# A row gradient on one core: six rows per partition over three tiles, and slots at multiples of 256 bytes

## The chip, the core and the metric

The kernel runs on one core of a Trainium2 chip. The metric is the device time of one execution in microseconds (us). Before the change the median of three runs was 1247.84 us, from 1247.62 to 1248.39.

## What is computed

The input is an 8192 x 8192 array of 32-bit floats. Each row is differentiated by itself:

```python
"x": np.random.randn(8192, 8192).astype(np.float32)

def reference(x):
    return np.gradient(x, axis=1)
```

Inside a row, the result at column j is half of x[j+1] - x[j-1]. At the two ends of a row it is the plain difference of the two outermost elements. 268.4 MB go in and 268.4 MB come out, and each element is used only within its own row.

## The kernel before

Memory on the core (SBUF) has 128 partitions. The 8192 rows are cut into 32 sets of 256 consecutive rows; each partition holds two consecutive rows of a set, 64 KiB that are contiguous in memory (HBM). The views of lines 36 and 37 do this cut: partition p of set s has rows 256 s + 2 p and 256 s + 2 p + 1. So the 128 pieces of one transfer lie end to end, and a transfer covers 8 MiB.

There are three slots in SBUF (line 40), each with 64 + 16,384 elements per partition. A set is loaded at element 64 of its slot (line 60). VectorE then writes half the difference of the neighbours to the same slot, 64 elements further down (line 76), so that it overwrites only what it has read. It runs over both rows as one stretch and leaves four wrong elements, at the ends of the two rows. GpSimd has put the right ones aside before (line 70, tile `ends`), and a small copy on VectorE or GpSimd sets them in place (line 87). The result is stored from element 0 of the slot (line 89).

All 64 transfers are issued by SyncE, in program order. Three loads come first. After each third set, the loads of the next three sets are issued (lines 91 to 93); each waits for the store that frees its slot (line 61). The order of SyncE is therefore: three stores, three loads, three stores, and so on; ten groups of three sets and a last one of two. The order of all engines is the one written out, and `chain` (line 45) names, for each instruction, the steps that it needs; other waits inside a slot are dropped as implied.

In the built program the first slot starts at byte 16,512 of each partition, which is 64 x 256 + 128; a slot is 65,792 bytes, 257 x 256, so the other two start 128 bytes past a multiple of 256 too.

Of the kernel before, what the change touches and what calls it, by code (L numbers as in the profile page):

```python
# [1 line left out]

# [4 lines left out]


@with_exitstack
def kernel(  # L10
    ctx: ExitStack,
    tc: tile.TileContext,
    x: bass.AP,
    out: bass.AP,
):

    nc = tc.nc
    P = nc.NUM_PARTITIONS
    n, m = x.shape
    R = 2
    NB = 3  # L30
    SH = 64
    W = R * m
    nsets = n // (P * R)
    f32 = x.dtype

    x_sets = x.rearrange("(s p t) m -> s p (t m)", p=P, t=R)
    out_sets = out.rearrange("(s p t) m -> s p (t m)", p=P, t=R)

    pool = ctx.enter_context(tc.tile_pool(name="pool", bufs=1))
    slots = [pool.tile([P, SH + W], f32, name=f"slot{k}", tag=f"slot{k}") for k in range(NB)]  # L40
    ends = pool.tile([P, nsets, R, 2], f32, name="ends", tag="ends")
    loads, stores = [], [None] * nsets
    in_front = {}

    def chain(i, ins, *needed):

        group, engine = f"slot{i % NB}", ins.ins.engine
        keep = [o.ins for o in needed]  # L50
        if in_front.get(engine, (None,))[0] == group:
            keep.append(in_front[engine][1])
        tc.declare_no_dep(ins.ins, group=group, keep=keep, reason="implied by the needed step")
        tc.add_to_no_dep_group(group, ins.ins)
        in_front[engine] = group, ins.ins
        return ins

    def load(i):
        b = slots[i % NB]
        ins = nc.sync.dma_start(out=b[:, SH : SH + W], in_=x_sets[i])  # L60
        loads.append(chain(i, ins, *([stores[i - NB]] if i >= NB else [])))

    with tc.manual_schedule():
        for i in range(NB):
            load(i)
        for i in range(nsets):
            b = slots[i % NB]
            xin = b[:, SH : SH + W].rearrange("p (t m) -> p t m", m=m)

            ins = nc.gpsimd.tensor_sub(  # L70
                out=ends[:, i, :, :],
                in0=xin[:, :, 1 : m : m - 2],
                in1=xin[:, :, 0 : m - 1 : m - 2],
            )
            at = [chain(i, ins, loads[i])]
            ins = nc.vector._custom_dve(  # L76
                dve_ops.TENSOR_TENSOR_REDUCE_SUB_MAX,
                out=b[:, 1 : W - 1],
                in0=b[:, SH + 2 : SH + W],
                in1=b[:, SH : SH + W - 2],  # L80
                s0=0.0,
                s1=0.5,
            )
            halved = chain(i, ins, *at)
            res = b[:, 0:W].rearrange("p (t m) -> p t m", m=m)
            placer = nc.gpsimd if i % 5 in (1, 3) and i < nsets - 2 else nc.vector
            ins = placer.tensor_copy(out=res[:, :, 0 : m : m - 1], in_=ends[:, i, :, :])  # L87
            placed = chain(i, ins, halved)
            ins = nc.sync.dma_start(out=out_sets[i], in_=b[:, 0:W])
            stores[i] = chain(i, ins, placed)  # L90
            if i % NB == NB - 1:
                for k in range(i + 1, min(i + 1 + NB, nsets)):
                    load(k)


# [1 line left out]
_INS = ['x']  # L97
_OUTS = [((8192, 8192), 'float32')]


# [23 lines left out]
```

## Time and profile before

| | us |
|---|---|
| median of three runs | 1247.84 |
| span of the profiled execution | 1245.7 |
| VectorE busy | 554.6 (45%) |
| GpSimd busy | 8.8 (1%) |
| one long VectorE operation (line 76) | 17.224 |
| one subtraction on GpSimd (line 70) | 0.198 |
| one copy of line 87 on VectorE, on GpSimd | 0.172, 0.190 |
| a load from issue to landing, median | 58.0 |
| a store from issue to landing, median | 40.4 |

The span runs from the first to the last instruction of the profiled execution, and the median of the runs is 2.1 us longer. The profile names engines as DVE (VectorE), POOL (GpSimd) and SP (SyncE); SPq is SyncE's queue of transfers. The time from issue to landing holds the wait behind the transfers that were issued earlier, since all share the same 16 DMA engines.

### The profile page before, as it was taken

The numbers are of one execution on the slowest core, as the hardware profiler recorded it, in microseconds if no ns is written. First come the engines' busy times: TensorE is split into PE (matmuls) and PEld (weight loads), VectorE is DVE, ScalarE is ACT, GpSimd is POOL, SyncE is SP. The second block draws the span as 40 slices with busy tenths as digits, with TensorE's granted clock in tenths as the row PEclk, the third lists the DMA queues.
The fourth block names the chain that finished last, engine by engine and source line by source line (L and its number), as shares of the span: only waits on it lengthen the run. The fifth ranks groups of instructions, "written<-read, shape, count | busy, mean of one in ns | idle before, by whom it ended". The sixth has DMA issues, their size and how long they took to land.

```text
span 1245.7 us, 237 instructions
## 1 busy us (share of the span) xinstructions
DVE 554.6 (45%) x52; POOL 8.8 (1%) x48
## 2 busy tenths in 40 slices
DVE  2850583069009702850582079009603840591083
POOL 0000000000000000000000000000000000000000
DMA  9999999999999999999999999999999999999999
GB/s 404 438 436 423 427 431 438 438 438 436 436 427 431 425 438 436 425 434 436 429 434 436 434 436 434 436 434 438 419 436 436 434 438 438 431 434 429 429 410 404
DMA packets 9217, 536.88 MB, mean 431 GB/s; under 512 B 1024, under 2 KB 1024, under 8 KB 1024
## 3 DMA queue, kind: packets, MB, share of 16 engines
q1 hardware_dynamic: 9216, 536.88, 99.8%
q14 instruction: 1, 0.01, 0.0%
HBM read 268.44 MB, written 268.44 MB: 431 GB/s over the span
## 4 chain that ended last, share of the span: by engine, by line
another core or an unknown queue 74%; DVE 18%; DMA 3%; issue 2%; POOL 1%; SPq 0%; POOLq 0%
DVE slot L76 18%; DMA slot<-in_x_dram 3%; POOL ends L70 0%; POOL slot L87 0%; SPq L60 0%; POOLq L119 0%; DVE slot L87 0%
## 5 line engine op out<-in xcount | busy, mean ns | idle before, releaser
L76 DVE CUSTOM_DVE_ANT_0 slot<-slot 128x16382 f32<-128x16382 f32 x32 | 551.2, 17224 | 668.7 <-POOL ends L70 668.7
L70 POOL TENSOR_TENSOR ends<-slot 128x4 f32<-128x4 f32 x32 | 6.3, 198 | 989.6 <-DMA slot<-in_x_dram 989.6
L87 POOL COPY slot<-ends 128x4 f32<-128x4 f32 x12 | 2.3, 190 | 207.9 <-DVE slot L76 207.9
L87 DVE COPY slot<-ends 128x4 f32<-128x4 f32 x20 | 3.4, 172 | 0.7
L108 POOL MEMSET const-bfloat16-1.0<- 128x1 bf16 x1 | 0.1, 101 | 0.0
L108 POOL MEMSET const-uint8-127<- 128x1 uint8 x1 | 0.1, 101 | 0.0
L108 POOL MEMSET const-float32-0.0<- 128x1 f32 x1 | 0.1, 98 | 0.2 <-issue 0.2
L108 POOL MEMSET const-float32-1.0<- 128x1 f32 x1 | 0.1, 98 | 0.0
## 6 DMA issues: line engine op xcount, KB each, us to landing
slot<-in_x_dram SPq DMA_DIRECT2D x32, 58.0
out_dram<-slot SPq DMA_DIRECT2D x32, 40.4
```

What stands on the lines that cost most here:

```text
L70: ins = nc.gpsimd.tensor_sub(out=ends[:, i, :, :], in0=xin[:, :, 1 : m : m - 2], in1=xin[:, :, 0 : m - 1 : m - 2],)
L76: ins = nc.vector._custom_dve(dve_ops.TENSOR_TENSOR_REDUCE_SUB_MAX, out=b[:, 1 : W - 1], in0=b[:, SH + 2 : SH + W], in1=b[:, SH : SH + W - 2],
L87: ins = placer.tensor_copy(out=res[:, :, 0 : m : m - 1], in_=ends[:, i, :, :])
L108: nc = _bacc.Bacc("TRN2", target_bir_lowering=False, num_devices=1)
```

## The change

The views of lines 36 and 37 are replaced by a function that cuts the rows in groups of three sets. A group is 768 consecutive rows, and each partition has six consecutive ones, 192 KiB. The first set of the group takes the first two rows of each partition, the second the next two, the third the last two. A transfer still moves 64 KiB for each of 128 partitions; its pieces now stand 192 KiB apart. The last group has two sets, with four rows per partition and a pitch of 128 KiB. The same cut is used for input and output.

A tile of 32 elements (128 bytes) per partition is placed ahead of the slots. Nothing reads or writes it. The first slot then starts at byte 16,640, 65 x 256, and the other two at multiples of 256 as well.

```diff
-    x_sets = x.rearrange("(s p t) m -> s p (t m)", p=P, t=R)
-    out_sets = out.rearrange("(s p t) m -> s p (t m)", p=P, t=R)
+    def sets(a):
+        found = []
+        for first in range(0, nsets, NB):
+            q = min(NB, nsets - first)
+            rows = a[first * P * R : (first + q) * P * R, :].rearrange("(p q) m -> p (q m)", p=P)
+            found += [rows[:, k * W : (k + 1) * W] for k in range(q)]
+        return found
+
+    x_sets, out_sets = sets(x), sets(out)
 
     pool = ctx.enter_context(tc.tile_pool(name="pool", bufs=1))
+    pad = pool.tile([P, 32], f32, name="pad", tag="pad")
     slots = [pool.tile([P, SH + W], f32, name=f"slot{k}", tag=f"slot{k}") for k in range(NB)]
```

## The prediction

> **What bounds the kernel now.** I read the page first, then SyncE's waits, then the timeline.
>
> ```profile
> DVE 554.6 (45%) x52; POOL 8.8 (1%) x48
> ...
> GB/s 404 438 436 423 427 431 438 438 438 436 436 427 431 425 438 436 425 434 436 429 434 436 434 436 434 436 434 438 419 436 436 434 438 438 431 434 429 429 410 404
> DMA packets 9217, 536.88 MB, mean 431 GB/s; under 512 B 1024, under 2 KB 1024, under 8 KB 1024
> ...
> q1 hardware_dynamic: 9216, 536.88, 99.8%
> ...
> another core or an unknown queue 74%; DVE 18%; DMA 3%; issue 2%; POOL 1%; SPq 0%; POOLq 0%
> ```
>
> The 16 DMA engines are occupied for 99.8% of the span, VectorE for 45%. The 74% that the chain of waits puts on an unknown queue is waiting for transfers. 9216 less 1024 small packets are 8192 of 64 KiB: 64 transfers x 128 partitions, one packet per partition and transfer.
>
> The timeline follows (start, time, engine, line, operation, idle time before it). The GpSimd subtraction of line 70 waits for a load, so its start marks a landing.
>
> ```profile
> 22.71 0.20 POOL L70 TENSOR_TENSOR ends<-slot 128x4 f32<-128x4 f32 x1 [22.27 <-DMA slot<-in_x_dram]
> ...
> 42.04 0.20 POOL L70 TENSOR_TENSOR ends<-slot 128x4 f32<-128x4 f32 x1 [19.13 <-DMA slot<-in_x_dram]
> ...
> 62.44 0.20 POOL L70 TENSOR_TENSOR ends<-slot 128x4 f32<-128x4 f32 x1 [2.69 <-DMA slot<-in_x_dram]
> ...
> 411.86 0.20 POOL L70 TENSOR_TENSOR ends<-slot 128x4 f32<-128x4 f32 x1 [19.85 <-DMA slot<-in_x_dram]
> ...
> 489.13 0.20 POOL L70 TENSOR_TENSOR ends<-slot 128x4 f32<-128x4 f32 x1 [59.56 <-DMA slot<-in_x_dram]
> ...
> 974.22 0.20 POOL L70 TENSOR_TENSOR ends<-slot 128x4 f32<-128x4 f32 x1 [19.15 <-DMA slot<-in_x_dram]
> 974.45 17.22 DVE L76 CUSTOM_DVE_ANT_0 slot<-slot 128x16382 f32<-128x16382 f32 x1 [1.92 <-POOL ends L70]
> 991.71 0.17 DVE L87 COPY slot<-ends 128x4 f32<-128x4 f32 x1
> 993.55 0.20 POOL L70 TENSOR_TENSOR ends<-slot 128x4 f32<-128x4 f32 x1 [19.13 <-DMA slot<-in_x_dram]
> ...
> 1206.28 0.20 POOL L70 TENSOR_TENSOR ends<-slot 128x4 f32<-128x4 f32 x1 [19.14 <-DMA slot<-in_x_dram]
> ```
>
> Two loads in a row land 993.55 - 974.22 = 19.33 us apart. Between 411.86 and 489.13 three stores and a load pass: 77.27 / 4 = 19.32 each. So loads and stores have one rate: 8.389 MB / 19.32 us = 434 GB/s. The compute of a set (0.20 + 17.22 + 0.17 us) fits beside one transfer, with the 1.92 us that VectorE idles to spare.
>
> This splits the profiled execution. 64 x 19.32 = 1236.5 us is pure transfer. Of the 1245.7 us span 9.2 are left: the first landing is 22.71 - 19.32 = 3.39 late (start); from there to the last landing 61 transfers should take 1178.5 us and take 1206.28 - 22.71 = 1183.57, 5.05 more; the two stores behind it should take 38.64 and take 1245.7 - 1206.28 = 39.42, 0.78 more. Most of the 5.05 sits in one place, the third load of each group, after which the queue turns from reading to writing: 62.44 - 42.04 = 20.40 us is 1.08 over 19.32. Over the ten full groups these excesses are 1.08, 0.13, 0.19, 0.73, 0.53, 0.47, 0.13, 0.52, 0.01 and 0.04, in all 3.8 us; the stretches of three stores and a load exceed 77.28 by about 1.0 in all, the second loads 19.32 by 0.25. Around the span lie 1247.84 - 1245.7 = 2.1 us that I carry over to the median.
>
> **What the change does, part by part.** The instructions stay: 32 loads, 32 stores, 32 subtractions, 32 long VectorE operations, 32 copies; the pad is written by none. The 64 issues by SyncE stay too, in their order.
>
> ```profile
> SPq L89 <- DVE slot L87: 525.6, 20, 55.9
> SPq L60 <- DMA out_dram<-slot: 373.1, 29, 19.3
> ```
>
> SyncE spends its time waiting for results and landed stores (us, times, longest), while a transfer or two still lie in the queue; an issue (0.34 us) is hidden behind them and would cost 64 x 0.34 = 22 us with that cover gone. Bytes per packet and packets per transfer stay as well. Two things move.
>
> First, **slot alignment**. A slot is 65,792 bytes, 257 x 256; the first starts at byte 16,512 of its partition, 128 past a multiple of 256. So now the SBUF side of every load and store is shifted by half of 256 bytes, and the pad (32 x 4 bytes) takes that away. The trace has no unshifted transfer, so bounds: if the shift costs nothing, 0. If it makes each packet pay for 128 bytes more, 128 / 65,536 of 1236.5 us, 2.4 us. That loads and stores both take 19.32 fits either end, since both touch the shifted side. A reason for a loss I don't see: a packet on a boundary has no piece more. I take the middle, -1.2.
>
> The Trainium skill ("DMA: Bandwidth & Descriptors", How a descriptor splits into AXI transactions) says that a read not starting on a multiple of 256 bytes begins at the boundary below and pays for the unused bytes. Its rule charges the read side, so stores alone, and by it the estimate would be half of the upper bound, 1.2 us. Equal rows for loads and stores speak against a charge on one side alone.
>
> Second, **row pitch**. A transfer's 128 pieces of 64 KiB lay end to end in HBM; now they stand 192 KiB apart and three transfers fill the gaps (the last group has two, pitch 128 KiB). A transfer's addresses then span 24 MiB, not 8. In the middle of a stretch of one direction nothing shows HBM as the limit: 19.32 us comes back for loads and stores, at the start and the end of the run. So I cost the steady stretches at 0. Where reads meet writes (the third load, the 3.8 us) the place in HBM can matter: now the last load of a group and the first store lie two sets, 16 MiB, apart in their tensors, then 128 KiB. Bounds: all 3.8 gone, or the stumble of the first group, 1.08, at all ten: 10.8 - 3.8 = +7.0. The present stumbles run from 0.01 to 1.08 at one pitch, so most of it has to do with how the engines happen to stand to one another, not with the addresses; the typical row (0.13 to 0.5) is nearer to none than to 1.08. I take -1.0, about a quarter of 3.8.
>
> Sum: 1245.7 - 1.2 - 1.0 = 1243.5 us of span, + 2.1 = **1245.6 us**.
>
> A gain at the third loads isn't eaten later: the queue has work until the last group, so a shorter third load lets every later landing move up. What is late next is the store of set 30, issued when its load has landed and 17.6 us of compute are done; both move up with it.
>
> **The rivals.**
>
> (a) The turnarounds go smooth: nearly all of the 3.8 vanishes, with 1.2 from alignment: 1247.84 - 5.0 = 1242.8 us. For it: reads and writes then differ in low address bits. Against: four groups already have under 0.15 without it.
>
> (b) Nothing that decides is touched: the 19.32 is the engines' own rate and the stumbles are chance: 1247.8 us. For it: the one rate in both directions. Against: only that two things do change on the path that sets the time.
>
> (c) Slower: the wider pitch puts the 16 streams in each other's way in HBM. Its place is the turn from loads to stores; priced as the first group's, 1.08 at each of ten, it gives 1247.84 + 7.0 = 1254.8 us. It decides, beyond 0.2%, from (3.8 + 2.5) / 10 = 0.63 us each, or in the steady stretch from 19.32 to 19.36 us per transfer (2.5 / 64 = 0.04). For it: stumbles of 1.08, 0.73 and 0.53 show that engines can hold each other up. Against: no steady stretch shows it.
>
> The Trainium skill ("DMA: Bandwidth & Descriptors", Latency and other measured facts, HBM row pitch) reports copies at a 512 KiB pitch at 207 GB/s per direction, 164 at 2 MiB, 103 at 4 MiB, against 214 at full rate. Were 192 KiB to cost what 512 KiB does there, the estimate would be 1236.5 x 7 / 207 = 42 us more; the present 64 KiB pitch runs without loss here, and no run shows a wider one.
>
> (d) Also slower: the row ranges of three stores now interleave, and if the program takes them as overlapping, each waits for the one before. The shortest store took 20.9 us from issue to landing, so 20.9 - 19.32 = 1.6 us of empty queue at two stores of each of ten groups and one of the last: 21 x 1.6 = 34 us, 1281 us. Against: the kernel names its waits, and only input, compute and slot are among them.
>
> **How the numbers follow.** My forecast 42%, (a) 23%, (b) 16%, (c) 15%, (d) 4%. A measurement of this kernel can tell about 0.2%, 2.5 us, from no change: faster is below 1245.3, slower above 1250.3. The forecast's own range, 1244.0 to 1247.5, lies on both sides: 18% of its 42 faster, 24 same. Faster 18 + 23 = 41%, same 24 + 16 = 40%, slower 19%. The range goes from 1241.5 ((a) with the upper bound of alignment, 1247.84 - 3.8 - 2.4 = 1241.6) to 1250.5, which leaves out most of (c), all of (d).
>
> **What would show it.** Landings of two loads in a row: 19.33 now; 19.29 if alignment is worth its full 2.4 us (2.4 / 64 = 0.04), 19.32 if nothing, over 19.36 if the pitch hurts. Third loads: the sum of their excess, 3.8 now, 2.8 by the forecast, near 0 by (a), 10 by (c). SyncE's waits of line 89 on a landed store would show (d). I am wrong in kind if the steady 19.32 moves by more than 0.04, and wrong in size if the third loads carry more than the 3.8 they have.

## The result: 1.9 us less, and the profile after

The changed kernel takes 1246.27 us (median of 21 runs, 1245.23 to 1247.13); the kernel before took 1248.16 us in the 21 runs beside them. The ratio is 0.9985, with a 95% interval from 0.9979 to 0.9991: a small gain, about 1.9 us. It is inside the 0.2% that the prediction counted as no change, but the interval does not reach 1, so the gain is real. The profiled execution has a span of 1244.3 us, 1.4 less than the one before.

The page of the changed kernel, with the lines that answer to those of before:

```profile
DVE 554.6 (45%) x52; POOL 8.9 (1%) x48
...
GB/s 404 438 436 423 421 438 438 438 438 436 434 423 430 434 438 438 430 436 432 428 434 436 432 436 434 438 436 430 432 428 438 436 434 438 434 434 430 430 409 404
DMA packets 9217, 536.88 MB, mean 431 GB/s; under 512 B 1024, under 2 KB 1024, under 8 KB 1024
...
q1 hardware_dynamic: 9216, 536.88, 99.8%
...
another core or an unknown queue 74%; DVE 18%; DMA 3%; issue 2%; POOL 1%; SPq 0%; POOLq 0%
```

Nothing has changed in kind: the same packets, the same work on the engines, the DMA engines occupied for 99.8%. The gain is too small for this page, so the landings have to be read one by one. The timeline of the changed kernel (start, time, engine, line, operation, idle time before it); what was line 70 is line 65 now:

```profile
22.77 0.20 POOL L65 TENSOR_TENSOR ends<-slot 128x4 f32<-128x4 f32 x1 [22.32 <-DMA slot<-in_x_dram]
...
42.03 0.20 POOL L65 TENSOR_TENSOR ends<-slot 128x4 f32<-128x4 f32 x1 [19.07 <-DMA slot<-in_x_dram]
...
62.34 0.20 POOL L65 TENSOR_TENSOR ends<-slot 128x4 f32<-128x4 f32 x1 [2.60 <-DMA slot<-in_x_dram]
...
410.87 0.20 POOL L65 TENSOR_TENSOR ends<-slot 128x4 f32<-128x4 f32 x1 [19.41 <-DMA slot<-in_x_dram]
...
488.16 0.20 POOL L65 TENSOR_TENSOR ends<-slot 128x4 f32<-128x4 f32 x1 [59.58 <-DMA slot<-in_x_dram]
...
972.75 0.20 POOL L65 TENSOR_TENSOR ends<-slot 128x4 f32<-128x4 f32 x1 [19.08 <-DMA slot<-in_x_dram]
...
992.06 0.20 POOL L65 TENSOR_TENSOR ends<-slot 128x4 f32<-128x4 f32 x1 [19.11 <-DMA slot<-in_x_dram]
...
1204.86 0.20 POOL L65 TENSOR_TENSOR ends<-slot 128x4 f32<-128x4 f32 x1 [19.07 <-DMA slot<-in_x_dram]
```

Three stores and a load between 410.87 and 488.16 take 77.29 us, 77.27 before. The first landing and the tail behind the last one (1244.3 - 1204.86 = 39.44 us, 39.42 before) are as they were. The difference lies between: from the first landing to the last the excess over 61 x 19.32 us is 3.57 us, where it was 5.05. Split as in the prediction: third loads of a group 3.34 (3.83 before), stretches of three stores and a load 0.32 (0.97), second loads -0.09 (0.25).

Are steady stores any faster now that they are read from a multiple of 256 bytes? SyncE issues three loads in a row, each behind a landed store, so the time from the first issue to the end of the third is two stores and an issue. One such line from the timeline before, and then one after:

```profile
1012.87 38.97 SPq L60 DMA_DIRECT2D slot<-in_x_dram  x3
```

```profile
1011.40 39.01 SPq L55 DMA_DIRECT2D slot<-in_x_dram  x3
```

They are not: 38.97 and 39.01. The packet records say it more sharply. In the steady stretches 16 packets are under way at any time; I joined each to the one that ends where it begins, so that a chain follows one of the 16 DMA engines. The median time from a packet to the one eight later is 19,319 ns, in the kernel before, in the changed one and in every kernel below at a pitch of 64 or 192 KiB with loads and stores in one queue. Inside the stretches of stores alone, and of loads alone, it is 19,319 ns too. So a shifted slot does not slow the steady transfers, and the gain comes from where the direction changes.

### The profile page after: what moved, and what is told of

Read it like the earlier page. It is cut to its first block, busy times and chain, and to the rows that moved or that the text cites. A ratio compares the mean times of both kernels' runs of the same rounds, so it can differ in the third digit from the quotient of the medians.

```text
span 1244.3 us, 237 instructions
## 1 busy us (share of the span) xinstructions
DVE 554.6 (45%) x52; POOL 8.9 (1%) x48
## 3 DMA queue, kind: packets, MB, share of 16 engines
q1 hardware_dynamic: 9216, 536.88, 99.8%
## 4 chain that ended last, share of the span: by engine, by line
another core or an unknown queue 74%; DVE 18%; DMA 3%; issue 2%; POOL 1%; SPq 0%; POOLq 0%
DVE slot L71 18%; DMA slot<-in_x_dram 3%; POOL ends L65 0%; POOL slot L82 0%; SPq L55 0%; POOLq L114 0%; DVE slot L82 0%
## 5 line engine op out<-in xcount | busy, mean ns | idle before, releaser
L71 DVE CUSTOM_DVE_ANT_0 slot<-slot 128x16382 f32<-128x16382 f32 x32 | 551.2, 17224 | 667.2 <-POOL ends L65 667.2
L65 POOL TENSOR_TENSOR ends<-slot 128x4 f32<-128x4 f32 x32 | 6.4, 200 | 988.1 <-DMA slot<-in_x_dram 988.1
```

The source lines that it names most:

```text
L65: ins = nc.gpsimd.tensor_sub(out=ends[:, i, :, :], in0=xin[:, :, 1 : m : m - 2], in1=xin[:, :, 0 : m - 1 : m - 2],)
L71: ins = nc.vector._custom_dve(dve_ops.TENSOR_TENSOR_REDUCE_SUB_MAX, out=b[:, 1 : W - 1], in0=b[:, SH + 2 : SH + W], in1=b[:, SH : SH + W - 2],
```

## The experiments

Every ratio is to the kernel before, run beside the experiment on the same chip, with its 95% interval. Theory A says that the row pitch brings the gain, theory B the slots' alignment.

**Each part alone.** The pad without the new cut:

```diff
     pool = ctx.enter_context(tc.tile_pool(name="pool", bufs=1))
+    pad = pool.tile([P, 32], f32, name="pad", tag="pad")
```

> The kernel before with the pad alone: slots on multiples of 256 bytes, transfers end to end as before. Theory A (the gain comes from the row pitch, at the turns between reading and writing): ratio 1.000, third loads' excess about 3.8 us as before. Theory B (the gain comes from the slots' alignment): ratio 0.9985, 1.9 us less than before. If the two share it, about 0.9992. In all cases two loads in a row stay 19.32 us apart.

Measured 1246.58 us, ratio 0.9991 (0.9982 to 1.0000). The new cut without the pad:

```diff
-    pad = pool.tile([P, 32], f32, name="pad", tag="pad")
```

> The changed kernel without the pad: pitch 192 KiB, slots 128 bytes past a multiple of 256. Theory A (pitch): ratio 0.9985. Theory B (alignment): 1.000. Shared: about 0.9992.

Measured 1247.75 us, ratio 1.0001 (0.9993 to 1.0010). And the changed kernel as it is, on the same chip:

> The changed kernel once more, beside the other three on one chip. Both theories: ratio 0.9985, 1246.3 us.

Measured 1245.88 us, ratio 0.9983 (0.9975 to 0.9992). Theory A in its plain form falls: the pitch alone brings nothing that shows. The pad alone brings about 1 us, though its interval reaches 1.0000, and the two together 1.8.

**The pad once more, and a worse shift.** Both kernels were repeated on another chip, to see whether the pad's gain holds and whether the pitch adds to it.

> The pad alone once more, on another day's chip beside the changed kernel. Theory B2: 0.999 again, 1246.6 us. Theory A2: 1.000. If the pitch adds on aligned slots, the changed kernel stays some 0.7 us below this one; if not, they are equal.

> The changed kernel, beside the pad alone: 0.9984. Equal to the pad alone if the pitch does nothing; 0.7 us below it if it adds.

Measured 1246.08 us for the pad alone, 0.9987 (0.9978 to 0.9995), and 1245.67 us for both, 0.9984 (0.9976 to 0.9993). The pad's gain holds. The 22 runs of the changed kernel on these two chips have a mean that is 0.68 us below that of the 22 runs of the pad alone, plus or minus 0.31 (1.96 standard errors of the difference): on aligned slots the pitch does add something. On shifted slots it did not show, though the interval there would allow 0.9 us.

Next, everything in the slots was moved by one element more, so that the SBUF side starts 132 bytes past a multiple of 256:

```diff
-    slots = [pool.tile([P, SH + W], f32, ...
+    slots = [pool.tile([P, SH + W + 64], f32, ...
...
-        b = slots[i % NB]
+        b = slots[i % NB][:, 1:]
...
-            b = slots[i % NB]
+            b = slots[i % NB][:, 1:]
```

> The kernel before with everything in the slots moved up by one element, so that the SBUF side of all transfers starts 132 bytes past a multiple of 256 and 4 past one of 32. Theory B2 (a shifted start makes the transfers uneven, so a worse shift costs at least as much): slower than before, or the same if only the multiple of 256 counts; steady transfers above 19.32 us if a start inside 32 bytes costs one step of the bus per packet. Theory A2 (alignment is worth nothing, the 0.9991 of the pad alone was chance): 1.000.

Measured 1247.61 us, ratio 1.0000 (0.9991 to 1.0008), and 19,319 ns per eight packets as ever. A start that is no multiple of 32 bytes costs no more, as far as these runs can tell, than one that is 128 past a multiple of 256. Other remainders than 0, 128 and 132 were not run.

**Which side of the transfers.** With 96 elements in place of 64 ahead of the data, loads and stores start at different remainders, so one can be aligned and the other not. First the loads:

```diff
-    SH = 64
+    SH = 96
...
-    slots = [pool.tile([P, SH + W], f32, ...
+    slots = [pool.tile([P, 128 + W], f32, ...
```

> The kernel before with SH 96 in place of 64: loads are written to a multiple of 256 bytes, stores are still read from 128 past one. If the writing of loads into SBUF carries the alignment's gain: ratio about 0.999, 1246.4 us, and 1.000 in the next run. If the reading of stores carries it (the rule that a read begins at the boundary below): 1.000 here.

Measured 1247.55 us, ratio 0.9999 (0.9990 to 1.0008). The same with the pad in front has the stores aligned and the loads not:

> The pad and SH 96: stores are read from a multiple of 256 bytes, loads are written 128 past one. If the reading side carries the gain: ratio about 0.999 here and 1.000 in the run with the loads aligned. If both sides share it: 0.9995 in each.

Measured 1246.62 us, ratio 0.9991 (0.9982 to 1.0000): as much as the pad alone gave on the first chip. This interval too reaches 1, but the two runs stand side by side on one chip, and the mean with the stores aligned is 0.98 us below the mean with the loads aligned, plus or minus 0.45. The reading of the stores carries the gain; how the loads are written makes no difference to the whole that shows. (With aligned stores VectorE's writes start on a multiple of 256 as well, but its long operation takes 17,224 ns in both runs, as before.) The row of the line-70 subtraction ends with GpSimd's whole wait for loads, which follows the time of the last landing. Kernel before, then loads aligned, then stores aligned (its line has moved to 71):

```profile
L70 POOL TENSOR_TENSOR ends<-slot 128x4 f32<-128x4 f32 x32 | 6.3, 198 | 989.6 <-DMA slot<-in_x_dram 989.6
```

```profile
L70 POOL TENSOR_TENSOR ends<-slot 128x4 f32<-128x4 f32 x32 | 6.4, 200 | 989.9 <-DMA slot<-in_x_dram 989.9
```

```profile
L71 POOL TENSOR_TENSOR ends<-slot 128x4 f32<-128x4 f32 x32 | 6.4, 200 | 988.7 <-DMA slot<-in_x_dram 988.7
```

The changed kernel and the pad alone have 988.1 in this row. But the pitch alone has 988.7 in it, as low as with the stores aligned, and its runs showed no gain: its profiled execution, 1246.71 us, was the fastest of its eleven. One profile can be off by as much as the gain, so the runs decide, and the profiles only help to say where. The excesses of the ten third loads, worked out from each timeline, fall into two groups. Where stores are read 128 or 132 bytes past a multiple of 256 (before, pitch alone, shift, loads aligned) they are 3.8, 3.6, 4.4 and 4.3 us; where they are read from a multiple (changed kernel three times, pad alone twice, stores aligned) 3.3, 3.3, 2.3, 3.2, 2.6 and 3.3. The means are 4.05 and 3.01, and the 1.0 between them is close to the gain of stores aligned alone (1.0 us). The stretches of three stores and a load seem to group by the pitch instead: 0.97, 0.42, 0.70, 0.93, 0.93 and 0.64 at 64 KiB, 0.39, 0.32, 0.03 and 0.13 at 192 KiB, on average 0.77 and 0.22, but 0.42 and 0.39 nearly touch. Each number is from one execution.

**Reads and writes side by side.** The changed kernel with loads on ScalarE's queue, so that there are no turns:

```diff
-        ins = nc.sync.dma_start(out=b[:, SH : SH + W], in_=x_sets[i])
+        ins = nc.scalar.dma_start(out=b[:, SH : SH + W], in_=x_sets[i])
...
-            if i % NB == NB - 1:
-                for k in range(i + 1, min(i + 1 + NB, nsets)):
-                    load(k)
+            if i + NB < nsets:
+                load(i + NB)
```

> The changed kernel with its loads issued by ScalarE, each as soon as its slot is free, so that loads and stores run side by side in two queues and there is no turn from reading to writing. If the turns cost what the third loads' excess shows (3.3 us) and mixing costs nothing: 1243 us. If reads and writes in flight together disturb each other all the time as they do at a turn (about 0.3 us per transfer): 64 x 0.3 = 19 us more, 1265 us.

Measured 1252.2 us (1248.28 to 1263.12), ratio 1.0050 (1.0031 to 1.0070): neither of the two. Its rate by slices:

```profile
GB/s 403 437 437 437 437 437 418 426 432 437 434 437 437 437 434 430 437 437 437 432 426 428 432 437 430 437 437 437 437 437 437 434 437 437 426 424 430 437 434 313
```

Of the 40 slices, 22 reach 437, so in this execution reads and writes in flight together do not slow each other steadily. What it loses here is at the end: 313 GB/s in the last slice, where the changed kernel has 404. At 31.2 us to a slice, (404 - 313) / 437 x 31.2 = 6.5 us. The packet records show why: the last load lands at 1209.76 us and its store is issued 17.7 us later, but the store before it is nearly done at 1221, so that few packets or none are under way until 1228. Whether mixing with a better end would beat the changed kernel was not tried, and why its runs differ by so much stays open.

**A wider pitch.** Does the pitch hurt at all, as rival (c) had it? All 32 sets in one group give each partition 64 consecutive rows, a pitch of 2 MiB:

```diff
-        for first in range(0, nsets, NB):
-            q = min(NB, nsets - first)
+        for first in range(0, nsets, nsets):
+            q = nsets
```

> The changed kernel with one group of all 32 sets: each partition has 64 consecutive rows, pitch 2 MiB, slots aligned. Theory A in its plain form (what matters is how far a read lies from a write at a turn, 128 KiB here as in the changed kernel): 0.9985. Rival (c) of the prediction, the pitch as such makes the 16 streams collide in HBM: steady transfers rise over 19.36 us, and the time over 1250 us; by the page's rule far over. Theory B (alignment alone): 0.9985 as well, unless the streams collide.

Measured 1303.56 us, ratio 1.0450 (1.0434 to 1.0467). Groups of eight sets give 512 KiB:

> The changed kernel with groups of eight sets: pitch 512 KiB, slots aligned. By the page's rule (207 against 214 GB/s) 3% slower, 1285 us; half way between 192 KiB (0.9984) and 2 MiB (1.045) by the logarithm of the pitch, 1.018. If the collision needs the full 2 MiB, where 128 partitions cover 256 MiB: as the changed kernel, 0.9984.

Measured 1258.55 us, ratio 1.0086 (1.0072 to 1.0099). The rate by slices, first at 2 MiB, then at 512 KiB:

```profile
GB/s 354 395 425 391 409 429 437 375 439 429 427 385 435 429 421 409 425 437 397 433 433 437 387 437 431 417 419 427 435 407 431 431 431 409 429 431 423 413 294 298
```

```profile
GB/s 400 433 433 400 433 431 433 400 433 431 433 404 433 429 433 427 423 431 421 431 427 435 425 433 427 433 433 433 427 433 433 433 436 435 433 429 433 437 392 400
```

At 512 KiB a slice of 400 or so comes back about every fourth slice, once per group, and fades after the third time. The landings say where it is: the ten stretches of three stores and a load take 79.9, 79.7, 78.9, 77.9, 78.1, 77.4, 77.3, 77.3, 77.3, 77.3 us, and the third loads are 9.1 us over in all, while two loads in a row stay 19.3 apart. At 2 MiB the stretches start at 83.1 and still take 79.7 in the last group. The timeline of its beginning:

```profile
27.15 0.20 POOL L65 TENSOR_TENSOR ends<-slot 128x4 f32<-128x4 f32 x1 [26.71 <-DMA slot<-in_x_dram]
...
48.89 0.20 POOL L65 TENSOR_TENSOR ends<-slot 128x4 f32<-128x4 f32 x1 [21.54 <-DMA slot<-in_x_dram]
...
70.30 0.20 POOL L65 TENSOR_TENSOR ends<-slot 128x4 f32<-128x4 f32 x1 [3.70 <-DMA slot<-in_x_dram]
...
153.43 0.20 POOL L65 TENSOR_TENSOR ends<-slot 128x4 f32<-128x4 f32 x1 [82.93 <-DMA slot<-in_x_dram]
```

The very first load lands at 27.15 instead of 22.77 us, the second 21.74 later, before there is any store: at this pitch reads alone are slow at the start. That streams which start together hold each other up is my reading of it, not shown. Later second loads are at 19.3 to 19.4 again. The end is slow too: the two stores behind the last landing take 50.2 us, where the changed kernel has 39.4. Last, the 2 MiB pitch for the input alone:

```diff
-    x_sets, out_sets = sets(x), sets(out)
+    x_sets = sets(x)
+    out_sets = out.rearrange("(s p t) m -> s p (t m)", p=P, t=R)
```

> Pitch 2 MiB for the input alone; the output keeps its contiguous sets, so its rows come in another order. If reading at that pitch is what costs, as long as 1303 us; if writing is (in the run with both, the stretches of three stores and a load took 79.6 to 83.1 us and single loads 19.3), close to the pad alone, 1246 to 1248 us.

Measured 1266.22 us, ratio 1.0148 (1.0133 to 1.0164): 18.6 us more than before, where both sides cost 55.9. So neither of the expectations holds; the input's pitch alone costs a third of that, and the rest appears only when the output has the pitch too. The output's pitch alone was not run. With the input alone the two stores behind the last landing take 39.5 us, so the slow end goes with the output.

The Trainium skill ("DMA: Bandwidth & Descriptors", Latency and other measured facts, HBM row pitch) has the direction right: it reports a loss at 512 KiB and a larger one at 2 MiB, and so do these runs. The size differs: by an estimate from its rates, 207 against 214 GB/s and 164 against 214 would be 3% and 30% longer, and this kernel lost 0.9% and 4.5%. Its copies run between HBM tensors in pieces of 16 KiB, the transfers here between HBM and SBUF in pieces of 64 KiB; which of the two makes the difference no run here shows. Nor do they show whether the size of the pitch counts or its being a power of two: 192 KiB is not one, 512 KiB and 2 MiB are, and no large pitch that isn't was run.

## Why the prediction was right, and where it was not

**What bounds the kernel**: right. Pure transfer of 64 x 19.32 us did not move, and all of the gain came out of the 9.2 us around it, as a gain had to if the steady rate held.

**Alignment, -1.2 us**: right in size by luck of the middle, wrong in place. The pad alone gave 1.1 and 1.75 us (medians on its two chips), stores aligned alone 1.0. But the term was worked out as 0 to 4.7 ns on each of 8192 packets, and the steady packets gained nothing at all; the profiles put the gain at the turn from loads to stores. The upper bound happened to be wide enough. The rule of the Trainium skill ("DMA: Bandwidth & Descriptors", How a descriptor splits into AXI transactions) that a read pays for an unaligned start got the side right: in these runs the gain follows the reading of stores, not the writing of loads. The runs don't bear out its charge per read, though. By an estimate from that rule every aligned store would be 1.2 / 32 us = 0.04 us shorter, and the eight packets take 19,319 ns either way. That the rule's total, 1.2 us, is close to what was measured is no proof of it. My argument from equal rows for loads and stores was thus right against a steady charge, and said nothing of the turns.

**Pitch, -1.0 us at the third loads**: direction right on aligned slots, place not borne out. There the pitch gave 0.7 us, but the third loads follow the alignment (4.05 against 3.01 us), not the pitch; the forecast had 2.8 us for them, and the three profiles of the changed kernel have 3.3, 3.3 and 2.3. That the term came out near its size is luck too. The profiles hint at the way back, the stretches of three stores and a load (0.8 to 0.2 on average). They don't show it: the pitch alone has a low number there, 0.39, and gained nothing in its runs. On shifted slots nothing showed.

**The sum**: 2.2 us were forecast and 1.9 measured. Neither term hid an error of the other; each came out near its size, but for another reason than supposed: the alignment gains at the turns and not in the steady transfers, and the pitch gained only once the slots were aligned.

**The rivals.** (a), smooth turns, did not happen: 3.3 of the 3.8 us at third loads are still there. (b), nothing at all, is what the pitch alone does as far as the runs can tell, but not the whole change. (c), a cost of a wider pitch, is real at 512 KiB and 2 MiB; at 192 KiB it doesn't show. At 512 KiB it sits about the turns: 9.1 us at the third loads, as supposed, and 8.2 more in the stretches of three stores and a load. At 2 MiB the third loads have only 7.6 us; the stretches have 36.0, and the rest is at the start and the end. That it comes from collisions in HBM is not shown. (d), stores waiting for each other, did not happen: SyncE waits 372.9 us for landed stores ahead of its loads, 373.1 before, and 20.3 us at the program's end in both; no store waits for another before it is issued.

**What stays open** is the mechanism at the turn: why the load ahead of a turn loses less when the stores behind it are read from a multiple of 256 bytes. The packet records show where the loss sits: in the last packet of each engine in the third load, just ahead of its first store packet. At the first turn of the kernel before, these 16 packets take 3.2 to 3.8 us in place of 2.42. Aligned stores leave that first turn nearly as it is (3.1 to 3.9 us with stores aligned alone). Over the ten turns together, an engine of the kernel before loses 3.2 us on average on such slow packets; it is 2.2 to 3.2 in the four profiles with shifted stores and 1.2 to 2.3 in the six with stores aligned, so the groups differ on average but overlap. That is where it happens, not why. Also open is why the pitch adds 0.7 us on aligned slots and nothing that shows on shifted ones.

## What to carry to other kernels

When the transfer queue is full from start to end, split the span into pure transfer and the rest before costing an edit: the rest is all that layout can win unless the steady rate itself moves, and here it was 9.2 of 1245.7 us. Read successive landings one by one; a gain of 0.15% is invisible in shares and rates and can be looked for in the ten places where the direction turns, but one profile is not enough for it. Start the SBUF side of stores on a multiple of 256 bytes where it costs only a pad: it was worth 1 to 1.75 of 1248 us here. Measure before using a pitch like 512 KiB or 2 MiB, which cost 0.9% and 4.5% here.

## What the runs showed that was not expected

At 512 KiB the pitch hurts most at the beginning: the stretches of three stores and a load fall from 79.9 to 77.3 us over the run without any change in the program. My reading, not tested, is that the engines drift apart and stop meeting. At 2 MiB it does not fade to nothing: the last stretch still takes 79.7 us. And where loads are written from a multiple of 256 bytes (changed kernel, pad alone, loads aligned) the second load of a group lands 19.27 and 19.37 us behind the first in turn, group by group, where it is 19.32 to 19.37 in no such order otherwise. The mean is 19.32 there and 19.34 otherwise, 0.25 us over the eleven groups, which the whole time of the run with loads aligned does not show.
